# A one-layer streaming encoder with 32 experts: early expert chunks through GpSimd's queue, two engines in written order around the router, section sums beside the experts

## The chip, the cores and the metric

The kernel runs on one core of a Trainium2 chip. The metric is device time in microseconds of one execution, the median of three runs. All data are float32 in HBM at the start; the weights (some 500 MB) are read once, and one output of 256 x 2048 is written.

## The reference

One layer on 256 tokens of width 2048. A vector `c` gives six rows of 2048 (two shifts, two scales, two gates) through `silu(c) @ w_ada`. Then:

```
x <- x + g1 * ([mLSTM heads || RG-LRU blocks](rmsnorm(x)*(1+sc1) + sh1) @ w_out)
h  = rmsnorm(x)*(1+sc2) + sh2
x <- x + g2 * HierMoE(h)
y  = rmsnorm(x) * final_g
```

HierMoE picks for every token one of 4 groups by a softmax and 2 of its 8 experts by another; an expert is `(silu(h @ gate) * (h @ up)) @ down` with width 512 inside, 12 MB of weights. Only experts that got tokens are loaded: here 112 chunks of 1 MiB for each of the three matrices, 28 experts.

## The kernel before, in words

**Order.** TensorE and SyncE run in the order in which the code is written (`manual_schedule`). VectorE, ScalarE and GpSimd are ordered by a scheduler that estimates when inputs are there. Every engine works off its own list strictly in order: an instruction that waits holds all that stand behind it. SyncE issues nearly all weight loads, GpSimd only two loads of `x` and some clearing.

**Chunks.** Weights come in chunks of 1 MiB (128 partitions x 4 x 512) into seven `ring` buffers, later with three `more` and three `early` ones. `chunk` (line 154) takes the next buffer and puts the load on SyncE's queue, where it waits until the buffer's last reader is done. `weights` (line 168) makes the loads of one expert; its first three chunks go to the `early` buffers (lines 180 to 186): a pair that takes the place of `XG`, and one that takes the place of `va_aug`.

**Stages.** After the input projection (until about 435 us) comes the output projection `w_out`: 16 chunks, each split into two float32r halves by ScalarE and VectorE (lines 465, 466) and multiplied on TensorE (lines 495 to 497), four chunks for each quarter `n` of the 2048 columns. Beside it `ada_later` (line 303) works off w_ada for the later sections, chunk by chunk: most on VectorE (line 325, into `acc`), the last six on TensorE (line 315); `acc_sum` and `ada_sum` (lines 281 to 301) add up a section. `step` and `fill` hand out such side work. Just before the projection of `n` = 0 and 1 goes on with its second half, SyncE's list has the three `early` loads (line 832), and GpSimd loads `x` again into `X1` (line 829) for the residual.

**From the last residual to the first expert.** `residual` (776) adds to `X1` and sums squares; `router` (784) transposes the normed rows and multiplies with the router's weights; `fill` (853) does the last six w_ada chunks; `r2` is the norm (ScalarE's Sqrt, line 344); VectorE finds the group and both experts by maxima (lines 866 to 925, ends in `MS`); `choice_weights` (905) is two softmaxes with ScalarE's Exp; ScalarE writes the normed rows `XN` (933); TensorE counts (`pcnt`, `ppre`, lines 966 to 974), VectorE turns this into ranks (`key`, `cmp`, `hot`) and positions (`pre`, `pos0`, one-hot matrices `two`, lines 940 to 942). `gather` (945) multiplies `XN` with `two` and copies the result to `XE` in four pieces of four columns, VectorE and ScalarE in turn (lines 955, 958).

**Experts.** Ten rounds of two to four experts (`experts`, 1072). Round 0 has the two busiest experts and its tokens' positions are known before the full ranking is. In a round, `prod` (1089) does the gate and up products, chunk by chunk; each frees its buffer, and SyncE then loads the next chunk into it. `begin` (1229) is side work in round 0: the rest of the first gather, tables, `g2_rows`.

Of the kernel before, what the change touches and what calls it, by code (L numbers as in the profile page):

```python
# [14 lines left out]
OP = mybir.AluOpType  # L15
AX = mybir.AxisListType

D = 2048
# [21 lines left out]
NB = 1 + sum(n for _, n in OVER)  # L40
OVER_AFTER = 5

FILL = 5

EARLY = (2,)

# [63 lines left out]
def block_kernel(ctx, tc, x, c, w_ada, b_ada, w_in, b_gates, vec_a, vec_b, w_lru_a, w_lru_x, w_out,  # L110
# [57 lines left out]
    def weights(e, by_f, cond=None):  # L168
        cache = {}

        def f(part, kk):
            if (part, kk) not in cache:
                if part == 2 and by_f:
                    s = w_e_down[e].rearrange("a (f p) (j n) -> p (a f) j n", p=128, j=4)[:, kk]
                elif part == 2:
                    s = w_e_down[e].rearrange("a (f p) n -> p (a f) n", p=128)[:, :, kk * 512:kk * 512 + 512]
                else:
                    s = (w_e_gate, w_e_up)[part][e].rearrange("a (k p j) n -> p (a k) j n", p=128, j=4)[:, kk]
                count[0] += 1
                if count[0] == 1:  # L180
                    pair = st([128, 2, 4, 512], "early", "S1")
                    held.extend((pair[:, 0], pair[:, 1], st([128, 4, 512], "early3", "V8")))
                if count[0] <= 3:
                    cache[part, kk] = held[count[0] - 1]
                    SP.dma_start(cache[part, kk], s)
                    return cache[part, kk]
                if count[0] == 4:
                    more = st([128, 2, 4, 512], "more", "S4")
                    ring.extendleft(more[:, i] for i in range(2))
                    ring.extend(held)  # L190
                if count[0] == 6:
                    ring.appendleft(st([128, 4, 512], "more3", "ws", 3))
                cache[part, kk] = chunk(s, cond)
            return cache[part, kk]
        return f
# [644 lines left out]
    for n in (2, 3):  # L840
        ps = [pa() for _ in range(2)]
        for kk in (2, 3, 0):
            w_out_chunk(ps, n, kk)
        g1 = gate_row(n)
        w_out_chunk(ps, n, 1)
        if n == 3:
            drain()
        residual(ps, n, g1)
        if n == 2:
            side.append(router(n))  # L850


# [2 lines left out]
            step()  # L855
            next(later, None)

    for i, _ in enumerate(router(3)):
        if i == 1:
            fill()  # L860
    fill(FILL)
    ssum = st([128, 2], "ssum")
    V.tensor_reduce(ssum, ss2, axis=AX.X, op=OP.add)
    r2 = rstd_of(ssum, D, "r2")
    for h in range(2):
        V.scalar_tensor_tensor(lg[:, h], plg[:, h], r2[:, h:h + 1], shw, op0=OP.mult, op1=OP.add)

# [94 lines left out]

    for kk in range(4):
        normed(kk)
    pcnt = pb([128, 33], name="pcnt")
    for h in range(2):
        PE.matmul(pcnt[:, 0:32], ones, MS[:, h], start=h == 0, stop=h == 1)
    for h in range(2):
        PE.matmul(pcnt[:32, 32:33], MS[:, h], ones[:, 0:1], start=h == 0, stop=h == 1)
    ppre = pb([128, 2, 32])  # L970
    lt = cs[:, C_LT:C_LT + 128]
    PE.matmul(ppre[:, 0], lt, MS[:, 0], start=True, stop=True)
    PE.matmul(ppre[:, 1], lt, MS[:, 1], start=True, stop=False)
    PE.matmul(ppre[:, 1], ones, MS[:, 0], start=False, stop=True)
    cnt = small([33], "cnt")
    tcopy(cnt[:, 0:32], pcnt[:, 0:32])
    keyc = st([32, 1], "keyc")
# [3 lines left out]
    V.tensor_tensor(key, key, cs[:, C_KEY + 32:C_KEY + 64], op=OP.add)  # L981
    cmp = st([32, 32], "cmp")
    V.tensor_scalar(cmp, key[:32], keyc, None, op0=OP.is_lt)
    pre = small([2, 32], "pre")
    tcopy(pre, ppre)

    pre0, posx, pos0 = small([2, 2], "pre0"), small([2, 2, 2], "posx"), small([2, 2], "pos0")
    V.tensor_tensor(pre0, pre[:, :, 0:2], cs[:, None, C_B0:C_B0 + 2].to_broadcast([128, 2, 2]), op=OP.add)
    V.scalar_tensor_tensor(pre0, pre[:, :, 0:2], 64.0, pre0, op0=OP.is_lt, op1=OP.mult)
    for i in range(2):  # L990
        V.tensor_tensor(posx[:, i], Mf[:, i, :, 0:2], pre0, op=OP.mult)
    V.tensor_reduce(pos0, posx, axis=AX.X, op=OP.add)
    gather0 = gather(one_hot(lambda i, h: pos0[:, i, h:h + 1], 1))
    prk = pb([32, 32])
    PE.matmul(prk, ones[:32, :32], cmp, start=True, stop=True)
    hot = st([32, 32], "hot")
    V.tensor_scalar(hot, prk, cs[:32, C_P:C_P + 1], None, op0=OP.is_equal)
    XE = next(gather0)
    ptab = pb([128, 3, 32])
    for i in range(3):  # L1000
        PE.matmul(ptab[:, i], cs[:32, C_TAB + 128 * i:C_TAB + 128 * i + 128], hot, start=True, stop=True)
# [9 lines left out]
    for i in range(2):  # L1011
        V.tensor_tensor(pm2[:, i], Mf[:, i], posf, op=OP.mult)
    PW = small([2, 2, 2], "PW")
    V.tensor_reduce(PW[:, 0], pm2, axis=AX.X, op=OP.add)
    choice_weights()
    tcopy(PW[:, 1], wt)
    posr = small([4, NR], "posr")
    V.tensor_tensor(posr, PW[:, 0].rearrange("p i h -> p (i h)")[:, :, None].to_broadcast([128, 4, NR]),
                    cs[:, None, C_RB:C_RB + NR].to_broadcast([128, 4, NR]), op=OP.subtract)
    fill(16)  # L1020

    drain()
    g2 = st([128, D], "g2", "acc")

    def g2_rows(n):
        A.activation(g2[:, n * 512:n * 512 + 512], bcast(ada[:, 5, n * 4:n * 4 + 4]), AF.Copy)

    eidf = st([32, 2], "eidf")
    j32 = st([32, 32], "j32")
# [42 lines left out]
    def experts(members, XE, Cw, done=None, ahead=iter(()), before=iter(()), by_member=False):  # L1072
# [23 lines left out]
        def combine(n, pd):  # L1096
            ns = slice(n * 512, n * 512 + 512)
            C, sw = Cw
            y = w2([128, 512], "y")
            V.scalar_tensor_tensor(y, pd, sw, g2[:, ns], op0=OP.mult, op1=OP.mult)  # L1100
            ys = [w2([128, 512], f"ys{i}", F32R) for i in range(2)]
            A.activation(ys[0], y, AF.Copy)  # L1102
            V.tensor_tensor(ys[1], y, ys[0], op=OP.subtract)
# [98 lines left out]
            V.tensor_scalar(oslot, oslot, 128.0, None, op0=OP.add)  # L1202

    ss3 = st([128, 2, 4], "ss3")
    s3 = st([128, 2], "s3")
    fg = {}

    def final_row(n, t):
# [20 lines left out]
    def begin():  # L1229
# [4 lines left out]
        next(gather0)  # L1234
        yield
        tables()
        yield
        for n in range(4):
            g2_rows(n)
# [78 lines left out]
```

## Time and profile before

| what | value |
|---|---|
| median of 3 runs | 1372.88 us (1371.62, 1372.88, 5239.75) |
| profiled execution | 1371.18 us, span on the core 1369.4 us |
| busy share of the span | TensorE 85%, VectorE 40%, ScalarE 26%, GpSimd 0% |
| mean DMA rate | 369 GB/s over the span |
| DMA on the chain that ended last | 18% of the span, its largest part |

The span is from the first to the last instruction; the execution's own time has 1.8 us more around it. A share over the whole span hides that the stages have different limits: where TensorE is busy all the time the DMA queues pause, and the other way round, so the stages have to be read apart.

### The profile page before, as it was taken

What the parts mean: (1) busy time and instruction counts of PE and PEld (TensorE: products, weight loads), DVE (VectorE), ACT (ScalarE), POOL (GpSimd) and SP (SyncE); (2) the same over time, 40 slices, a digit from 0 to 9 for tenths busy, and PEclk for the clock granted to TensorE, in tenths of its full rate; (3) what the DMA queues carried; (4) which work ended last, traced back from release to release, by engine and by line L of the source; (5) the groups of instructions that cost most, each with busy time, mean ns of one, the idle gap of its engine ahead of it and who ended that gap; (6) DMA issues with size and microseconds to landing.
All of it is one profiled execution on the core that took longest, in us unless ns stands there. A gap on an engine that the chain in (4) does not pass through costs nothing. (4 is left out here: it accounts for less than half of the span.)

```text
span 1369.4 us, 20227 instructions
## 1 busy us (share of the span) xinstructions
PE 1170.4 (85%) x8186; PEld 682.6 (50%) x8186; DVE 545.6 (40%) x990; ACT 351.6 (26%) x562; POOL 4.0 (0%) x10
## 2 busy tenths in 40 slices
PE   4898999999999799699996878968885778887886
PEld 1666889988799678444431323313341133421432
DVE  1333666779769678422230131301331013130214
ACT  2233594545436344421010100101010010100103
POOL 0000000000000000000000000000000000000000
PEclk9999999999999899899999999999997899998998
DMA  9999869688968898879999999999997999999995
GB/s 337 367 356 364 269 225 346 243 319 316 400 250 330 343 376 324 338 286 389 423 422 423 424 423 423 423 424 422 423 423 320 423 423 424 422 423 424 423 414 218
DMA packets 116897, 504.84 MB, mean 369 GB/s; under 512 B 12424, under 2 KB 14760, under 8 KB 69184
## 3 DMA queue, kind: packets, MB, share of 16 engines
q1 hardware_dynamic: 115264, 500.11, 91.5%
q0 software_dynamic: 288, 2.10, 0.4%
q8 instruction: 66, 1.08, 0.3%
q10 hardware_dynamic: 1248, 1.29, 0.3%
q14 instruction: 31, 0.25, 0.0%
HBM read 526.54 MB, written 2.10 MB: 386 GB/s over the span
## 5 line engine op out<-in xcount | busy, mean ns | idle before, releaser
L1091 PE MATMUL pa<-ring,XE 128*32 128x512 f32 x1376 | 226.7, 630 | 56.8 <-DMA ring<-in_w_e_up_dram 28.5
L481 PE MATMUL pa<-HH,ws 128*128 128x256 f32 x640 | 189.6, 296 | 3.5 <-ACT ws L465 1.9
L483 PE MATMUL pa<-HH,ws 128*128 128x256 f32 x640 | 186.0, 291 | 5.2 <-DVE ws L466 5.2
L482 PE MATMUL pa<-HL,ws 128*128 128x256 f32 x640 | 185.8, 290 | 1.4 <-DVE HL L376 1.4
L466 DVE TENSOR_TENSOR ws<-ring,ws 128x1024 fp32r<-128x1024 f32 x128 | 154.6, 1220 | 70.1 <-ACT ws L465 65.4
L465 ACT ACTIVATE ws<-ring 128x1024 fp32r<-128x1024 f32 x128 | 134.1, 1058 | 171.9 <-PE pa L483 106.6
L1091 PE MATMUL pa<-early,XE 128*32 128x512 f32 x656 | 131.8, 622 | 25.9 <-DMA early<-in_w_e_up_dram 19.0
L1091 PEld LDWEIGHTS pa<-ring,XE 128*32 128x32 f32 x1376 | 60.3, 114 | 184.4 <-issue 99.0
L481 PEld LDWEIGHTS pa<-HH,ws 128*128 128x128 f32 x640 | 127.4, 199 | 19.6 <-issue 8.4
L483 PEld LDWEIGHTS pa<-HH,ws 128*128 128x128 f32 x640 | 127.3, 199 | 6.7 <-DVE ws L466 6.7
L482 PEld LDWEIGHTS pa<-HL,ws 128*128 128x128 f32 x640 | 127.4, 199 | 2.1 <-DVE HL L376 1.9
L955 ACT ACTIVATE XE<-pb,adx 128x128 f32<-128x128 f32 x80 | 36.6, 457 | 313.9 <-DVE XE L958 313.9
L1091 PE MATMUL pa<-more,XE 128*32 128x512 f32 x528 | 105.9, 609 | 12.8 <-DMA more<-in_w_e_up_dram 12.8
L1144 PE MATMUL pa<-ring,hT 128*32 128x512 f32 x616 | 102.1, 605 | 10.9 <-DMA ring<-in_w_e_down_dram 10.8
L1123 DVE TENSOR_TENSOR hs<-hs,pa 128x512 f32<-128x512 f32 x10 | 6.9, 688 | 260.9 <-PE pa L1091 260.9
L325 DVE SCALAR_TENSOR_TENSOR acc<-ring,cz,acc 128x1024 f32<-128x1024 f32 x80 | 100.3, 1277 | 0.8 <-DMA ring<-in_w_ada_dram 0.8
L1111 DVE TENSOR_TENSOR X<-X,pa 128x512 f32<-128x512 f32 x80 | 52.0, 683 | 93.9 <-PE pa L1109 93.9
L951 PE MATMUL pb<-two,XN 128*128 128x128 f32 x640 | 80.6, 286 | 8.0 <-ACT hT L1130 6.7
L951 PEld LDWEIGHTS pb<-two,XN 128*128 128x128 f32 x640 | 76.2, 198 | 19.4 <-issue 10.6
L1091 PEld LDWEIGHTS pa<-early,XE 128*32 128x32 f32 x656 | 32.0, 113 | 90.1 <-issue 41.8
L1102 ACT ACTIVATE ys<-y 128x512 fp32r<-128x512 f32 x40 | 25.2, 630 | 180.4 <-DVE y L1100 180.4
L1144 PE MATMUL pa<-more,hT 128*32 128x512 f32 x328 | 60.3, 594 | 5.4 <-DMA more<-in_w_e_down_dram 5.4
(369 smaller groups left out, 1267.5 us busy)
## 6 DMA issues: line engine op xcount, KB each, us to landing
ring<-in_w_ada_dram SPq DMA_DIRECT2D x96, 1024.0 KB
ring<-in_w_e_up_dram SPq DMA_DIRECT2D x61, 1024.0 KB
ring<-in_w_e_down_dram SPq DMA_DIRECT2D x60, 1024.0 KB
ring<-in_w_e_gate_dram SPq DMA_DIRECT2D x59, 1024.0 KB
ring<-in_w_in_dram SPq DMA_DIRECT2D x48, 1024.0 KB
early<-in_w_e_up_dram SPq DMA_DIRECT2D x30, 1024.0 KB
more<-in_w_e_down_dram SPq DMA_DIRECT2D x30, 1024.0 KB
more<-in_w_e_gate_dram SPq DMA_DIRECT2D x27, 1024.0 KB
```

What stands on the lines that cost most here:

```text
L325: V.scalar_tensor_tensor(o, w[:, h:h + 2], cz[:, k, 3:4], o, op0=OP.mult, op1=OP.add)
L465: A.activation(ws[:, 0], s, AF.Copy)
L466: V.tensor_tensor(ws[:, 1], s, ws[:, 0], op=OP.subtract)
L481: PE.matmul(o, wh[:, cc], HH[:, k], start=k == 0 and ch % 2 == 0, stop=False, skip_group_check=True)
L482: PE.matmul(o, wh[:, cc], HL[:, k], start=False, stop=False, skip_group_check=True)
L483: PE.matmul(o, wl[:, cc], HH[:, k], start=False, stop=k == 15, skip_group_check=True)
L951: PE.matmul(p[:, j], XN[:, h, kk, j], which[:, h], start=h == 0, stop=h == 1)
L955: A.activation(XE[:, k], p[:, j], AF.Identity, scale=adx[:, 1, k:k + 1], bias=adx[:, 0, k:k + 1])
L1091: PE.matmul(o[c0:c0 + width], lhs(kk, j)[:, c0:c0 + width], w[:, j], start=first and j == 0, stop=last and j == 3)
L1102: A.activation(ys[0], y, AF.Copy)
L1111: V.tensor_tensor(X1[:, h, ns], X1[:, h, ns], pc, op=OP.add)
L1144: PE.matmul(pds[n][c0:c0 + width], hT[:, f, c0:c0 + width], w[:, n], start=f == 0, stop=f == 3)
```

## The change

The first three expert chunks are issued by GpSimd in place of SyncE. The last `residual`, the last router quarter, the argmaxima, ranks, positions and choice weights are written out in a new order, and ScalarE and VectorE take that order as written (`in_order`); `choice_weights` moves behind the positions, `ppre` ahead of `pcnt`, the first one-hot ahead of the ranks. A Sqrt on a constant is written ahead of the last residual. Of the last six w_ada chunks four are worked off before the logits are scaled, two behind the counts (`FILL`). The sum of the last section (`acc_sum`, `ada_sum`) and the buffer `g2` move into `begin`, beside round 0.

```diff
--- before.py
+++ after.py
@@ -40,7 +40,7 @@
 NB = 1 + sum(n for _, n in OVER)
 OVER_AFTER = 5
 
-FILL = 5
+FILL = (4, 2)
 
 EARLY = (2,)
 
@@ -182,7 +182,7 @@
                     held.extend((pair[:, 0], pair[:, 1], st([128, 4, 512], "early3", "V8")))
                 if count[0] <= 3:
                     cache[part, kk] = held[count[0] - 1]
-                    SP.dma_start(cache[part, kk], s)
+                    G.dma_start(cache[part, kk], s)
                     return cache[part, kk]
                 if count[0] == 4:
                     more = st([128, 2, 4, 512], "more", "S4")
@@ -843,10 +843,8 @@
             w_out_chunk(ps, n, kk)
         g1 = gate_row(n)
         w_out_chunk(ps, n, 1)
-        if n == 3:
-            drain()
-        residual(ps, n, g1)
         if n == 2:
+            residual(ps, n, g1)
             side.append(router(n))
 
 
@@ -855,13 +853,32 @@
             step()
             next(later, None)
 
-    for i, _ in enumerate(router(3)):
-        if i == 1:
-            fill()
-    fill(FILL)
+    drain()
+    in_order = tc.manual_schedule(engines={mybir.EngineType.Activation, mybir.EngineType.DVE})
+    in_order.__enter__()
+
+    s3 = st([128, 2], "s3")
+    A.activation(s3, epsc, AF.Sqrt, scale=0.0, bias=eps)
+    residual(ps, 3, g1)
+    pxs = [pb([128, 2, S]) for _ in range(2)]
+    xts = [w2([128, 2, S], "xt") for _ in range(2)]
+    for i in range(2):
+        for j in range(2):
+            k = 12 + i * 2 + j
+            for h in range(2):
+                PE.transpose(pxs[i][:, j, h * 128:h * 128 + 128], X1[:, h, k * 128:k * 128 + 128], ident)
+    V.tensor_tensor(xts[0], pxs[0], ada[:, 4, 12:14, None].to_broadcast([128, 2, S]), op=OP.mult)
     ssum = st([128, 2], "ssum")
     V.tensor_reduce(ssum, ss2, axis=AX.X, op=OP.add)
     r2 = rstd_of(ssum, D, "r2")
+    for j in range(2):
+        A.activation(xts[1][:, j], pxs[1][:, j], AF.Copy, scale=ada[:, 4, 14 + j:15 + j])
+    for i in range(2):
+        for j in range(2):
+            for h in range(2):
+                PE.matmul(plg[:, h], xts[i][:, j, h * 128:h * 128 + 128], wr[:, 12 + i * 2 + j], start=False,
+                          stop=i == 1 and j == 1, skip_group_check=True)
+    fill(FILL[0])
     for h in range(2):
         V.scalar_tensor_tensor(lg[:, h], plg[:, h], r2[:, h:h + 1], shw, op0=OP.mult, op1=OP.add)
 
@@ -962,16 +979,27 @@
 
     for kk in range(4):
         normed(kk)
+    ppre = pb([128, 2, 32])
+    lt = cs[:, C_LT:C_LT + 128]
+    PE.matmul(ppre[:, 0], lt, MS[:, 0], start=True, stop=True)
+    PE.matmul(ppre[:, 1], lt, MS[:, 1], start=True, stop=False)
+    PE.matmul(ppre[:, 1], ones, MS[:, 0], start=False, stop=True)
     pcnt = pb([128, 33], name="pcnt")
     for h in range(2):
         PE.matmul(pcnt[:, 0:32], ones, MS[:, h], start=h == 0, stop=h == 1)
     for h in range(2):
         PE.matmul(pcnt[:32, 32:33], MS[:, h], ones[:, 0:1], start=h == 0, stop=h == 1)
-    ppre = pb([128, 2, 32])
-    lt = cs[:, C_LT:C_LT + 128]
-    PE.matmul(ppre[:, 0], lt, MS[:, 0], start=True, stop=True)
-    PE.matmul(ppre[:, 1], lt, MS[:, 1], start=True, stop=False)
-    PE.matmul(ppre[:, 1], ones, MS[:, 0], start=False, stop=True)
+    fill(FILL[1])
+    pre = small([2, 32], "pre")
+    tcopy(pre, ppre)
+
+    pre0, posx, pos0 = small([2, 2], "pre0"), small([2, 2, 2], "posx"), small([2, 2], "pos0")
+    V.tensor_tensor(pre0, pre[:, :, 0:2], cs[:, None, C_B0:C_B0 + 2].to_broadcast([128, 2, 2]), op=OP.add)
+    V.scalar_tensor_tensor(pre0, pre[:, :, 0:2], 64.0, pre0, op0=OP.is_lt, op1=OP.mult)
+    for i in range(2):
+        V.tensor_tensor(posx[:, i], Mf[:, i, :, 0:2], pre0, op=OP.mult)
+    V.tensor_reduce(pos0, posx, axis=AX.X, op=OP.add)
+    hot0 = one_hot(lambda i, h: pos0[:, i, h:h + 1], 1)
     cnt = small([33], "cnt")
     tcopy(cnt[:, 0:32], pcnt[:, 0:32])
     keyc = st([32, 1], "keyc")
@@ -981,21 +1009,12 @@
     V.tensor_tensor(key, key, cs[:, C_KEY + 32:C_KEY + 64], op=OP.add)
     cmp = st([32, 32], "cmp")
     V.tensor_scalar(cmp, key[:32], keyc, None, op0=OP.is_lt)
-    pre = small([2, 32], "pre")
-    tcopy(pre, ppre)
-
-    pre0, posx, pos0 = small([2, 2], "pre0"), small([2, 2, 2], "posx"), small([2, 2], "pos0")
-    V.tensor_tensor(pre0, pre[:, :, 0:2], cs[:, None, C_B0:C_B0 + 2].to_broadcast([128, 2, 2]), op=OP.add)
-    V.scalar_tensor_tensor(pre0, pre[:, :, 0:2], 64.0, pre0, op0=OP.is_lt, op1=OP.mult)
-    for i in range(2):
-        V.tensor_tensor(posx[:, i], Mf[:, i, :, 0:2], pre0, op=OP.mult)
-    V.tensor_reduce(pos0, posx, axis=AX.X, op=OP.add)
-    gather0 = gather(one_hot(lambda i, h: pos0[:, i, h:h + 1], 1))
+    gather0 = gather(hot0)
+    XE = next(gather0)
     prk = pb([32, 32])
     PE.matmul(prk, ones[:32, :32], cmp, start=True, stop=True)
     hot = st([32, 32], "hot")
     V.tensor_scalar(hot, prk, cs[:32, C_P:C_P + 1], None, op0=OP.is_equal)
-    XE = next(gather0)
     ptab = pb([128, 3, 32])
     for i in range(3):
         PE.matmul(ptab[:, i], cs[:32, C_TAB + 128 * i:C_TAB + 128 * i + 128], hot, start=True, stop=True)
@@ -1012,18 +1031,17 @@
         V.tensor_tensor(pm2[:, i], Mf[:, i], posf, op=OP.mult)
     PW = small([2, 2, 2], "PW")
     V.tensor_reduce(PW[:, 0], pm2, axis=AX.X, op=OP.add)
-    choice_weights()
-    tcopy(PW[:, 1], wt)
     posr = small([4, NR], "posr")
     V.tensor_tensor(posr, PW[:, 0].rearrange("p i h -> p (i h)")[:, :, None].to_broadcast([128, 4, NR]),
                     cs[:, None, C_RB:C_RB + NR].to_broadcast([128, 4, NR]), op=OP.subtract)
-    fill(16)
-
-    drain()
-    g2 = st([128, D], "g2", "acc")
+    choice_weights()
+    tcopy(PW[:, 1], wt)
+    in_order.__exit__(None, None, None)
+
+    g2 = []
 
     def g2_rows(n):
-        A.activation(g2[:, n * 512:n * 512 + 512], bcast(ada[:, 5, n * 4:n * 4 + 4]), AF.Copy)
+        A.activation(g2[0][:, n * 512:n * 512 + 512], bcast(ada[:, 5, n * 4:n * 4 + 4]), AF.Copy)
 
     eidf = st([32, 2], "eidf")
     j32 = st([32, 32], "j32")
@@ -1097,7 +1115,7 @@
             ns = slice(n * 512, n * 512 + 512)
             C, sw = Cw
             y = w2([128, 512], "y")
-            V.scalar_tensor_tensor(y, pd, sw, g2[:, ns], op0=OP.mult, op1=OP.mult)
+            V.scalar_tensor_tensor(y, pd, sw, g2[0][:, ns], op0=OP.mult, op1=OP.mult)
             ys = [w2([128, 512], f"ys{i}", F32R) for i in range(2)]
             A.activation(ys[0], y, AF.Copy)
             V.tensor_tensor(ys[1], y, ys[0], op=OP.subtract)
@@ -1202,7 +1220,6 @@
             V.tensor_scalar(oslot, oslot, 128.0, None, op0=OP.add)
 
     ss3 = st([128, 2, 4], "ss3")
-    s3 = st([128, 2], "s3")
     fg = {}
 
     def final_row(n, t):
@@ -1234,6 +1251,9 @@
         next(gather0)
         yield
         tables()
+        fill()
+        drain()
+        g2.append(st([128, D], "g2", "acc"))
         yield
         for n in range(4):
             g2_rows(n)
```

The order of instructions shows what becomes of it on three places. SyncE, where the output projection's second half begins (the difference; `ring` buffers are the chunks):

```order
 L158 DMA ring_65<-in_w_out_dram 128x4x512
 L158 DMA ring_66<-in_w_ada_dram 128x2048
-L185 DMA early<-in_w_e_gate_dram 128x2048 x2
-L185 DMA early_3863<-in_w_e_gate_dram 128x2048
 L158 DMA ring_67<-in_w_out_dram 128x4x512
 L158 DMA ring_68<-in_w_ada_dram 128x2048
```

The three `early` loads are gone from SyncE's list; the next `w_out` chunk follows at once. GpSimd after the change, from the clearing of `brow` to the branch after the rounds (`early_3863` is the buffer in `va_aug`'s place, `X_3859` is `X1`):

```order
L215 MEMSET brow 128x512 x4
L185 DMA early_3863<-in_w_e_gate_dram 128x2048
L185 DMA early<-in_w_e_gate_dram 128x2048
L829 DMA X_3859<-in_x_dram 128x2048 x2
L185 DMA early<-in_w_e_gate_dram 128x2048
L1208 TENSOR_LOAD on
```

Before, the two loads of `X1` stood alone there. Now two `early` loads stand ahead of them and one behind.

VectorE behind the choice of the experts, before (`MS` is the last of the choice, `gss` to `p` the choice weights):

```order
L925 TENSOR_TENSOR MS<-M 128x64
L886 TENSOR_REDUCE gss<-gp 128x2
L886 TENSOR_REDUCE ess<-ep 128x2
L887 RECIPROCAL gss<-gss 128x2
L887 RECIPROCAL ess<-ess 128x2
L888 TENSOR_TENSOR gp<-gp,gss 128x8
L888 TENSOR_TENSOR ep<-ep,ess 128x16
L910 TENSOR_REDUCE pg<-gp 128x2
L911 TENSOR_REDUCE p_4642<-ep 128x2
L912 TENSOR_TENSOR ept<-ep,h_4525 128x16
```

and after:

```order
L942 TENSOR_TENSOR MS<-M 128x64
L135 COPY pre<-pb 128x64
L997 TENSOR_TENSOR pre_4572<-pre,cs 128x4
L998 SCALAR_TENSOR_TENSOR pre_4572<-pre,pre_4572 128x4
L1000 TENSOR_TENSOR posx<-M,pre_4572 128x4 x2
L1001 TENSOR_REDUCE pos_4574<-posx 128x4
L958 TENSOR_SCALAR one<-cs,pos_4574 128x128
L959 SCALAR_TENSOR_TENSOR two<-cs,pos_4574,one 128x128
L958 TENSOR_SCALAR one<-cs,pos_4574 128x128
L959 SCALAR_TENSOR_TENSOR two<-cs,pos_4574,one 128x128
L135 COPY cnt<-pcnt 128x32
L1006 TENSOR_SCALAR keyc<-pcnt,cs 32x1
```

The softmax sums, which read ScalarE's Exp, stood right behind `MS`; now positions and one-hot matrices (`one`, `two`) stand there, and the ranks (`cnt`, `keyc`) behind them. The choice weights stand 36 rows behind `MS`, between copies of `XE`. The Sqrt on a constant (line 861) needs nothing that comes late, and stands on ScalarE right behind its first activation of the program, not at the last residual; the table load of line 344 is still there, now ahead of the second pair of `xt` copies, one of which pairs has moved to VectorE (line 870).

TensorE, from the ranks to the first expert, before (`acc` and `row` are the section's sum):

```order
L995 MATMUL pb<-cmp,cs 32x32
L951 MATMUL pb<-two,XN 128x128 x8
L1001 MATMUL pb<-hot,cs 128x32 x3
L285 MATMUL pa<-acc,cs 32x512 x4
L298 MATMUL pb<-cs,row 128x4 x4
L951 MATMUL pb<-two,XN 128x128 x8
L1091 MATMUL pa<-early,XE 32x512 x16
```

and after:

```order
L968 MATMUL pb<-two,XN 128x128 x8
L1015 MATMUL pb<-cmp,cs 32x32
L1020 MATMUL pb<-hot,cs 128x32 x3
L968 MATMUL pb<-two,XN 128x128 x8
L1109 MATMUL pa<-early,XE 32x512 x16
L968 MATMUL pb<-two,XN 128x128 x8
```

The section's sum is gone from here (it now stands in round 0 behind the third pair of gate chunks and the tables), and the first gather stands ahead of the rank's product.

## Rows read from the trace of the kernel before

**Rows 1.** the page, a group: busy us, mean ns; idle before, releaser.

```profile
L955 ACT ACTIVATE XE<-pb,adx 128x128 f32<-128x128 f32 x80 | 36.6, 457 | 313.9 <-DVE XE L958 313.9
```

**Rows 2.** busy time by stretch (us): engines (xcount), then PEclk, DMA share, GB/s.

```profile
442.50:445.00 2.50, 2.50 (x14) 2.08 (x13) 2.32 (x5) 1.86 (x3) 0.00 (x0) 1.00 0.01 3
460.00:468.00 8.00, 0.65 (x4) 0.20 (x2) 0.03 (x1) 1.12 (x2) 0.00 (x0) 0.69 1.03 424
553.00:586.00 33.00, 22.39 (x144) 15.27 (x144) 15.67 (x88) 16.11 (x23) 0.00 (x0) 0.74 0.71 290
575.00:590.00 15.00, 14.12 (x90) 10.09 (x91) 5.35 (x25) 1.83 (x4) 0.00 (x0) 0.75 0.12 51
710.00:1040.00 330.00, 258.50 (x1816) 99.34 (x1812) 70.01 (x146) 29.04 (x56) 0.00 (x0) 0.95 1.01 421
```

**Rows 3.** SyncE's queue in order of time: start us, us, what.

```profile
449.30 1.28 SPq L185 DMA_DIRECT2D early<-in_w_e_gate_dram  x3
450.63 0.64 SPq L158 DMA_DIRECT2D ring<-in_w_out_dram  x1
...
589.66 5.88 SPq L158 DMA_DIRECT2D early<-in_w_e_up_dram  x3
```

**Rows 4.** what SyncE's queue waited for: us in total, times, longest us.

```profile
SPq L185 <- PE pb L656: 10.6, 1, 10.6
```

**Rows 5.** TensorE in order of time, output projection; in brackets idle before, releaser.

```profile
467.99 0.79 PE L495 MATMUL pa<-ws,YM 128*128 128x512 f32 x1 [7.35 <-ACT ws L465]
...
473.52 0.39 PE L495 MATMUL pa<-ws,YM 128*128 128x512 f32 x1
...
476.29 0.60 PE L338 MATMUL pb<-cs,ada 128*128 128x128 f32 x4
...
483.66 0.50 PE L497 MATMUL pa<-ws,YM 128*128 128x512 f32 x1 [0.85 <-DVE ws L466]
```

**Rows 6.** DMA issues: count, KB each, median us from issue to landing.

```profile
X<-in_x_dram POOLq DMA_DIRECT2D x2, 1024.0 KB, 10.6
```

**Rows 7.** TensorE in order of time, from the router to the first experts.

```profile
574.78 3.75 PE L951 MATMUL pb<-two,XN 128*128 128x128 f32 x16 [1.30 <-DVE two L942]
578.46 1.16 PE L1001 MATMUL pb<-hot,cs 32*128 32x32 f32 x6
579.55 1.07 PE L285 MATMUL pa<-acc,cs 128*32 128x512 f32 x8
581.50 1.06 PE L298 MATMUL pb<-cs,row 128*128 128x4 f32 x8 [0.88 <-DVE row L292]
582.42 3.64 PE L951 MATMUL pb<-two,XN 128*128 128x128 f32 x16
585.99 3.64 PE L1091 MATMUL pa<-early,XE 128*32 128x512 f32 x32
589.56 2.05 PE L951 MATMUL pb<-two,XN 128*128 128x128 f32 x16
```

**Rows 8.** ScalarE in order of time, same stretch.

```profile
555.71 0.84 ACT L795 ACTIVATE xt<-pb,ada 128x256 f32<-128x256 f32 x2
556.57 1.28 ACT L344 ACT_TABLE_LOAD   x1
...
568.48 1.28 ACT L884 ACT_TABLE_LOAD   x1
```

**Rows 9.** VectorE in order of time, same stretch.

```profile
560.43 0.42 DVE L866 SCALAR_TENSOR_TENSOR lg<-pa,r,shw 128x36 f32<-128x36 f32 x2 [2.08 <-PE pa L802]
...
565.00 0.23 DVE L925 TENSOR_TENSOR MS<-M 128x64 f32<-128x64 f32 x1
570.02 0.16 DVE L886 TENSOR_REDUCE gss<-gp 128x2 f32<-128x8 f32 x1 [4.79 <-ACT gp L884]
...
572.16 0.18 DVE L135 COPY cnt<-pcnt 128x32 f32<-128x32 f32 x1
...
574.30 0.60 DVE L942 SCALAR_TENSOR_TENSOR two<-cs,pos,one 128x128 f32<-128x128 f32 x2
```


## The prediction, made before the changed kernel ran

> **What bounds the kernel now.** I read the page, then the busy time by stretch, then the three engines and SyncE's queue in order of time where a stretch showed idle DMA. All is one profiled execution, 1371.2 us, of which 1369.4 are the span; the median of the three runs, 1372.9, is 1.7 above it. The sum is made against 1371.2.
>
> Most of the second half is the experts' weights. From 710 to 1040 us the DMA queues are full all the time, 421 GB/s, and TensorE is busy for 258.5 of 330 us [rows 2]. There nothing that an engine does counts; the end is the time at which this stream begins, plus its bytes. What counts is therefore when the buffers begin to come free for it, and where DMA stood still before. It does so twice.
>
> The first place is in the output projection: from 442.5 to 445 us the queues move 3 GB/s, while TensorE has no idle time [rows 2]. SyncE waits there 10.6 us for one thing, the buffer pair of the first expert chunks, which TensorE's line 656 still reads [rows 4]. Not until 449.30 does it issue these loads and, right behind them, the next chunk of w_out [rows 3]. The price comes 15 us later: TensorE sits 7.35 us until 467.99 because that chunk is late [rows 5], and DMA runs at full rate meanwhile [rows 2].
>
> The second place is the router. From 575 to 590 us the queues move 51 GB/s [rows 2], which against 421 is 13.2 us of standstill: all buffers hold chunks of round 0, and the next load waits until the first pair of them is used, at 589.66 [rows 3, 7]. In the 33 us from 553 to 586 TensorE is busy for 22.4 and its mean granted clock is 0.74 [rows 2]. The chain goes logits (560.43), choice (to 565.23), then VectorE waits 4.79 us for an Exp of the choice weights [rows 9], because ScalarE writes eight normed pieces first and then loads a table, at 568.48 [rows 8]; then the choice weights, ranks and positions follow, and the first gather starts at 574.78 [rows 7].
>
> **Term 1: early chunks through GpSimd.** SyncE's list loses three loads and their wait. When it comes free in the trace it issues the next w_out chunk only 0.05 us after the early ones [rows 3], so a buffer was free for it; in the change it goes out when SyncE reaches it, some 10 us earlier, into queues that stand still. It was 7.4 us late; so it is there in time. What TensorE gets back: the 7.35 us; the half clock behind that wait (the first 12 matmuls take 467.99 to 473.52, 5.53 us, the second 12 take 2.77 [rows 5], so 2.8 us); and the 0.85 us at 483.66, where a split stood behind the residual on VectorE and now stands ahead of it [rows 5]. Together 11.0 us. GpSimd's queue pays: `X1` is loaded behind one early chunk. The nearest row is `X1` itself, two loads that landed after 10.6 us beside a full SyncE queue [rows 6]; a third at the same pace, 15.9 us from 449.3, ends at 465, and the residual that needs `X1` begins some 11 us earlier than in the trace, after 472. So this stays hidden, with about 7 us to spare. Lower end of the term: only the issue time of 1.28 us [rows 3]; upper end 11.0, since nothing else of TensorE's is idle there. I take 11.0, since the idle queues and the wait are both in the rows.
>
> For this I weighed a rule. The Trainium skill ("DMA: Bandwidth & Descriptors", section "Issuing engines are not separate DMA queues") says that loads issued from several engines run on the same 16 DMA engines, and that starting them elsewhere saves only the time of issue, usually small. Here the rows disagree as to what is saved: the issue is small, but the wait ahead of it held a whole list.
>
> **Term 2: from the last residual to the first expert.** Four steps.
> (a) Logits. The table load of the norm ran at 556.57, behind two copies of router columns, 0.84 us [rows 8]. In the new order it stands right behind the squares, and one pair of copies is VectorE's. The second pair, and with it the last router product, is earlier by about that, and 0.2 more since nothing stands between: the logits come at 559.4 in place of 560.43, 1.0. That the Sqrt on a constant ends up at the start of the program costs and brings nothing here, as the load no longer stands behind anything; I set it to 0.
> (b) Choice to one-hot. Before, 9.7 us lie between the end of `MS` (565.23) and the end of the one-hot (574.90) [rows 9]: 4.79 waiting, 2.1 of choice weights, 2.7 from the first copy of the counts at 572.16 on [rows 9]. Now the wait and the choice weights are behind. What is left: the `ppre` product, which now comes first on TensorE, 1.0, and of the 2.7 about 2.5, as the rank's steps no longer lie between. 3.5 in place of 9.7: 6.2.
> (c) Clock. Both gathers before the first expert took 3.75 and 3.64 us; the third one, of the same size, took 2.05 [rows 7], because TensorE had sat idle before the rank product and the granted clock was low (0.75 from 575 to 590 [rows 2]). Without the long wait TensorE has w_ada products and counts to fill the time, and I take 2.05 for both: 1.7 and 1.6.
> (d) The section's sum (1.07, a wait of 0.88, 1.06 [rows 7]) no longer stands there: 3.0. Against it: the table product (1.16 [rows 7]) now waits for `hot`, which VectorE makes behind two copies of `XE`, and for the first gather's buffer, free after four copies; these go in turn at 0.46 [rows 1], 1.9 in all, with only the short rank product beside them: costs 1.7.
> Sum 1.0 + 6.2 + 3.3 + 1.3 = 11.8: the first expert matmul comes 21.2 in place of 33.0 us after the last w_out one. Bounds: without the clock 8.5. Upwards DMA ends it: its standstill of 13.2 us [rows 2] is all that can be won.
>
> **Term 3: the section's sum beside round 0.** It stands behind the third pair of gate chunks, so TensorE frees the later buffers 2.1 us later, plus a wait for the row, 0.9 as before: 3.0 [rows 7]. The queues are nearly, but not always, busy there, so it can be hidden in part; 0 to 4, I take 2.9. The choice weights' place in VectorE's list, between copies of `XE`, I set to 0: a piece of `XE` is wanted one pair of products (3.64) and one gather (2.05) [rows 7] after its own gather, and its copies (1.9), one-hot steps (1.1) and a table load of 1.28 [rows 8] fit into that.
>
> **Sum.** 1371.2 - 11.0 - 11.8 + 2.9 = 1351.3; a median lies a little above a profile here, so I say 1352. From the ends: 11.0 + 13.2 - 0 gives 1347.0; 1.3 + 8.5 - 4 gives 1365.4. Two per cent, about what one takes as a clear difference here, is 27.5 us.
>
> **Rivals.**
> *The rule holds* (only issue time saved; the bytes are the limit). The early chunks and `X1`, 5 MB, then still stand ahead of w_out's chunks. Then 1371.2 - 1.3 - 8.9 = 1361. For it: behind 450 us DMA is full for long. Against: 3 GB/s before [rows 2]. 0.15. This is what the rule of the Trainium skill ("DMA: Bandwidth & Descriptors") in term 1 comes to.
> *The choice weights come back on the path.* VectorE and ScalarE are bound to the written order; softmax, Exp and copies of `XE` wait for each other, and TensorE waits in round 0 for `XE`. Price: up to the 6.9 us of before (4.79 and 2.1 [rows 9]), less the spare time of 1.4: 5.5. 1357. For it: two engines, one list each, a table load between two copies. 0.12.
> *Slower.* `X1` starves. Its loads stand on GpSimd's queue behind an early chunk and beside SyncE's full queue; if they land late, VectorE stops at the residual's addition (line 781), and behind it stand the splits for which TensorE waits. Every us after 472 is lost, and from 20 us on, a landing after 492, the kernel is slower than before; 25 us late gives 1376, and slower by 2% needs 47. A landing at 492 means 14 us a load, where two took 10.6 [rows 6]. The Trainium skill ("DMA: Bandwidth & Descriptors", section "SWDGE vs HWDGE vs iDMA") says that GpSimd writes its descriptors into SBUF, out of which VectorE's two-port mode locks it; no row shows that it held the two loads of before. 0.04, and 0.02 of it beyond 2%.
> *It does not do what it says:* the chain is limited elsewhere, for instance a clock that stays low, and DMA finds its standstill again; 1364 to 1372. 0.04.
> *More than I see:* the section's sum is hidden, and round 0 runs without DMA pauses; below 1345.4, over 2% faster. 0.05.
> The forecast, 1347 to 1357, has 0.60.
>
> So the range is 1346 to 1361.5: it leaves out the slow cases, the largest gain and half of the first rival. Faster by over 2%: 0.05, rounded up to 0.06 for what I may have mis-sized; slower by over 2%: 0.02; within: 0.92.
>
> **What would show it.** Term 1: no DMA standstill at 442.5 to 445 of the length of before, no TensorE wait of 7 us for a w_out chunk, the last w_out matmul at about 542 in place of 553. Term 2: the first expert matmul about 21 us behind it, the choice weights' sums behind the one-hot, both gathers at about 2 us. Term 3: lines 285 and 298 in round 0 with a short wait between. Wrong would be: VectorE stopping at line 781 until `X1` lands; TensorE waiting for `XE` in round 0; or DMA idle as long as before ahead of the first freed buffer.

## The result, and the profile after

The changed kernel takes 1352.51 us (median of four runs, 1352.37 to 1355.04), the kernel before 1371.62 beside it (median of three runs, 1371.36 to 1372.88; a fourth, of 5239.75 us, is left out here, but was counted in the median of 1372.88 us at the start). The ratio of the times is 0.9863, with a 95% interval from 0.9843 to 0.9882. It is 19.1 us or 1.4% faster: measurable, and under the 2% of a clear difference. The profiled execution has a span of 1350.3 us, 19.1 less than before. I forecast 1352.

The total alone says little on why. I cut the span at three events that stand in every trace: SyncE issues the first w_out load, the last w_out matmul starts (line 497), and SyncE issues the first load into a freed `early` buffer (the last row of [rows 3]). SyncE's queue of the changed kernel in order of time (start us, us, what):

```profile
414.10 0.38 SPq L158 DMA_DIRECT2D ring<-in_w_out_dram  x1
...
432.40 0.43 SPq L158 DMA_DIRECT2D ring<-in_w_out_dram  x1
...
566.56 5.88 SPq L158 DMA_DIRECT2D early<-in_w_e_up_dram  x3
```

The load at 432.40 is the w_out chunk that stood behind the three early loads, at 450.63 in [rows 3]: counted from the first w_out load it goes out 14.9 us sooner. The same queue before, and TensorE's last w_out row before:

```profile
417.40 0.38 SPq L158 DMA_DIRECT2D ring<-in_w_out_dram  x1
```

```profile
552.61 0.39 PE L497 MATMUL pa<-ws,YM 128*128 128x512 f32 x1
```

| stretch | before | after | difference | forecast |
|---|---|---|---|---|
| A: start to the first w_out load | 417.4 | 414.1 | -3.3 | 0 |
| B: to the last w_out matmul | 135.2 | 125.2 | -10.0 | -11.0 (term 1) |
| C: to the first freed buffer | 37.05 | 27.2 | -9.8 | -11.8 (term 2) |
| D: to the end of the span | 779.7 | 783.7 | +4.0 | +2.9 (term 3) |

**B.** TensorE has no wait of 7 us any more; before, that was the first row of [rows 5]. GpSimd's queue (start us, us, what; in brackets idle before, releaser):

```profile
409.11 0.66 POOL L185 DMA_DIRECT2D early<-in_w_e_gate_dram  x1 [34.72 <-ACT ws L465]
446.26 0.53 POOL L185 DMA_DIRECT2D early<-in_w_e_gate_dram  x1 [36.49 <-DVE TO L657]
448.74 1.05 POOL L829 DMA_DIRECT2D X<-in_x_dram  x2 [1.95 <-DVE YM L659]
```

GpSimd stands 36.5 us for the buffer pair, and nobody waits for GpSimd. SyncE issues w_out chunks meanwhile, and the standstill of [rows 2] (3 GB/s) is gone, as the busy time by stretch shows (length, engines with xcount, then PEclk, DMA share, GB/s):

```profile
440.00:445.00 5.00, 5.00 (x25) 4.08 (x25) 5.00 (x9) 3.01 (x6) 0.00 (x0) 1.00 0.82 283
445.00:450.00 5.00, 5.00 (x26) 4.12 (x25) 5.00 (x10) 2.92 (x4) 1.79 (x4) 1.00 1.03 393
...
540.00:545.00 5.00, 3.35 (x15) 2.86 (x16) 2.78 (x6) 3.77 (x9) 0.00 (x0) 0.71 1.00 423
545.00:550.00 5.00, 5.00 (x27) 2.79 (x30) 2.42 (x13) 5.00 (x5) 0.00 (x0) 0.50 0.49 208
```

Before, the standstill filled a whole stretch of this length:

```profile
445.00:450.00 5.00, 5.00 (x27) 4.15 (x26) 5.00 (x10) 3.05 (x5) 0.00 (x0) 1.00 0.01 3
```

w_out chunks are still late at ScalarE, which splits them, three times and 9.0 us in all, but TensorE has earlier chunks to multiply. The longest of the three:

```profile
465.46 1.06 ACT L465 ACTIVATE ws<-ring 128x1024 fp32r<-128x1024 f32 x1 [4.33 <-DMA ring<-in_w_out_dram]
```

**C and D.** TensorE from the end of w_out on, the answer to [rows 7]:

```profile
539.33 0.39 PE L497 MATMUL pa<-ws,YM 128*128 128x512 f32 x1
540.71 0.30 PE L869 MATMUL pb<-cs,X 128*128 128x128 f32 x1 [0.99 <-DVE X L781]
541.95 1.63 PE L869 MATMUL pb<-cs,X 128*128 128x128 f32 x7 [0.94 <-DVE X L781]
543.50 3.63 PE L879 MATMUL pa<-wr,xt 128*128 128x36 f32 x16
547.07 6.25 PE L315 MATMUL pa<-ring,cz 128*32 128x512 f32 x32
553.24 0.41 PE L984 MATMUL pb<-MS,cs 128*128 128x32 f32 x2
...
556.43 2.05 PE L968 MATMUL pb<-two,XN 128*128 128x128 f32 x16
...
560.13 0.85 PE L1020 MATMUL pb<-hot,cs 32*128 32x32 f32 x6 [1.48 <-DVE hot L1017]
560.91 2.05 PE L968 MATMUL pb<-two,XN 128*128 128x128 f32 x16
562.90 3.64 PE L1109 MATMUL pa<-early,XE 128*32 128x512 f32 x32
...
578.74 1.06 PE L285 MATMUL pa<-acc,cs 128*32 128x512 f32 x8
580.78 1.03 PE L298 MATMUL pb<-cs,row 128*128 128x4 f32 x8 [0.97 <-DVE row L292]
```

And VectorE there, the answer to [rows 9]:

```profile
547.17 0.42 DVE L883 SCALAR_TENSOR_TENSOR lg<-pa,r,shw 128x36 f32<-128x36 f32 x2 [2.72 <-PE pa L879]
...
551.74 0.22 DVE L942 TENSOR_TENSOR MS<-M 128x64 f32<-128x64 f32 x1
554.13 0.22 DVE L135 COPY pre<-pb 128x64 f32<-128x64 f32 x1 [2.18 <-PE pb L986]
...
565.47 0.16 DVE L903 TENSOR_REDUCE gss<-gp 128x2 f32<-128x8 f32 x1 [0.56 <-ACT gp L901]
```

The choice weights are behind the one-hot now (565.47), both gathers take 2.05 us in place of 3.75 and 3.64, and lines 285 and 298 stand in round 0. But there is something new: from 545 to 550 us TensorE's clock is at the lower of its two levels (0.50), and the four w_ada chunks of line 315 take 6.25 us for 32 matmuls, whereas 16 of them cost 1.9 at the full clock. They last until 553.2. `MS` is ready at 551.96, and the prefix product (line 984), for which VectorE waits 2.18 us, stands behind them.

DMA's standstill ahead of the first freed buffer is nearly gone: in the 15 us up to it the queues moved 60 GB/s before and 393 now. A shorter one is new: from 547.5 to 550 us they move nothing, since SyncE waits up to 11.1 us for `ring` buffers that line 315 reads at the low clock.

### The profile page after: what moved, and what is told of

It reads as the page before. It is cut to its first block, busy times and chain, and to the rows that moved or that the text cites. A ratio compares the mean times of both kernels' runs of the same rounds, so it can differ in the third digit from the quotient of the medians.

```text
span 1350.3 us, 20232 instructions
## 1 busy us (share of the span) xinstructions
PE 1166.2 (86%) x8186; PEld 678.3 (50%) x8186; DVE 547.7 (41%) x991; ACT 351.4 (26%) x561; POOL 5.6 (0%) x13
## 5 line engine op out<-in xcount | busy, mean ns | idle before, releaser
L968 PE MATMUL pb<-two,XN 128*128 128x128 f32 x640 | 77.3, 279 | 6.7 <-ACT hT L1148 6.7
L968 PEld LDWEIGHTS pb<-two,XN 128*128 128x128 f32 x640 | 73.1, 192 | 18.9 <-issue 9.2
```

Of the source, the lines that this page charges most:

```text
L968: PE.matmul(p[:, j], XN[:, h, kk, j], which[:, h], start=h == 0, stop=h == 1)
```

## The experiments

All twelve in the four stretches, from one profile each (us), with the ratio to the kernel before from the timed runs:

| kernel | A | B | C | D | ratio, 95% interval |
|---|---|---|---|---|---|
| before | 417.4 | 135.2 | 37.05 | 779.7 | |
| before, second profile | 417.0 | 135.2 | 37.0 | 780.3 | 1.0000 (0.9988 to 1.0012) |
| changed | 414.1 | 125.2 | 27.2 | 783.7 | 0.9863 (0.9843 to 0.9882) |
| changed, second profile | 414.5 | 125.2 | 27.2 | 783.5 | 0.9870 (0.9855 to 0.9886) |
| 1 GpSimd alone | 416.05 | 125.2 | 35.7 | 781.0 | 0.9894 (0.9878 to 0.9910) |
| 2 SyncE again | 416.1 | 135.3 | 27.2 | 783.3 | 0.9946 (0.9932 to 0.9959) |
| 3 no early Sqrt | 415.1 | 125.3 | 27.2 | 784.7 | 0.9878 (0.9863 to 0.9893) |
| 4 early Sqrt alone | 417.2 | 135.2 | 37.0 | 780.1 | 1.0005 (0.9996 to 1.0013) |
| 5 sum ahead | 416.7 | 125.2 | 32.5 | 781.0 | 0.9888 (0.9873 to 0.9903) |
| 6 choice first | 414.3 | 125.25 | 36.1 | 783.15 | 0.9930 (0.9917 to 0.9944) |
| 7 fill ahead | 417.6 | 125.25 | 26.7 | 784.8 | 0.9863 (0.9848 to 0.9878) |
| 8 sum in the gap | 417.6 | 125.2 | 27.1 | 781.75 | 0.9856 (0.9841 to 0.9871) |
| 9 fill before the choice | 414.0 | 125.5 | 29.0 | 784.0 | 0.9870 (0.9855 to 0.9885) |
| 10 fill and sum | 415.1 | 125.3 | 24.85 | 782.1 | 0.9844 (0.9826 to 0.9862) |

Where the program of a whole stretch is the same, B and C repeat within 0.4 us and D within 1.6. So B and C tell single microseconds apart, which D and the medians do not.

**1. GpSimd alone**, on the kernel before:

```diff
-                    SP.dma_start(cache[part, kk], s)
+                    G.dma_start(cache[part, kk], s)
```

> The kernel before with one edit: GpSimd issues the three early expert chunks. Theory (the wait ahead of the chunks held SyncE's whole list): TensorE's wait of 7.35 us for a w_out chunk is gone, the last w_out matmul ends some 10 us earlier, the first expert matmul still comes 33 us after it, and the kernel is 10 us faster, ratio 0.993. Rival (only the time of issue is saved, the bytes still stand ahead of w_out's chunks): 1.3 us, ratio 0.999. Rival (the gain is given back in the standstill of DMA from 575 to 590 us): TensorE's wait goes, the time stays, ratio 1.000.

1357.47 us against 1371.49. B is 10.0 shorter, as in the changed kernel, and C stays near that of before (1.4 shorter; the wait for the Exp is 2.79 us in place of the 4.79 of [rows 9], because the scheduler now puts VectorE's copies of the counts ahead of the choice weights, which the one line changed as well). The theory holds: the spans differ by 11.5 us, -10.0 in B, -1.4 each in A and C, +1.3 in D. (The medians differ by 14.0; the profiled run is the slowest of its five.) DMA's standstill of [rows 2] doesn't take the gain back.

**2. SyncE again**, on the changed kernel: the same line, the other way.

> The changed kernel with one edit undone: SyncE issues the three early chunks again. Theory (the parts add up): TensorE waits again some 7 us for a w_out chunk, w_out ends some 10 us later, the first expert matmul still comes 23.5 us behind it, and the kernel is 10 us slower than the changed one, 0.993 of the kernel before. Rival (the early chunks decide only the issue time): 1 us slower than the changed one, 0.987.

1363.76 us. B is back at 135.3, C and D are those of the changed kernel. TensorE's two waits of [rows 5] are back:

```profile
466.53 0.79 PE L495 MATMUL pa<-ws,YM 128*128 128x512 f32 x1 [7.25 <-ACT ws L465]
482.38 0.50 PE L497 MATMUL pa<-ws,YM 128*128 128x512 f32 x1 [0.85 <-DVE ws L466]
```

So the parts add up, and the first is worth 10.0 by both runs. The Trainium skill's rule ("DMA: Bandwidth & Descriptors", section "Issuing engines are not separate DMA queues"), that another issuing engine saves the issue time alone, would have given 1.3; these traces differ from it by what stood behind the wait.

**3 and 4. Without the early Sqrt, and that alone.** Stretch A came out 3.3 us shorter, though nothing of the change was meant for it; the one instruction that moved there is the Sqrt on a constant.

```diff
-    A.activation(s3, epsc, AF.Sqrt, scale=0.0, bias=eps)
```

> The changed kernel without the Sqrt on a constant, which runs at the program's start. In the changed kernel's trace all work up to the first w_out load is already 3.3 us earlier than before. Theory A (this Sqrt does it: its table is loaded while ScalarE idles, and the norm of the input comes 1.3 us less late): w_out's first load is issued at 417.4 us in place of 414.1, and the kernel is 3 us slower than the changed one, 0.989 of the kernel before. Theory B (the stretches of half clock in the input projection fall as they fall): 414.1 or anything between, unrelated to this edit.

> The kernel before with one edit: the Sqrt on a constant at the program's start. Theory A (this Sqrt brings the 3.3 us): w_out's first load is issued at 414.1 us in place of 417.4, and the kernel is 3 us faster, ratio 0.998. Theory B (chance of the clock): no difference from before, ratio 1.000, or one that does not match the edit.

Without it A is 415.1, not 417.4; alone it gives 417.2 and 1371.84 us, the time of before. The Sqrt is not the cause.

**The two kernels again**, unaltered.

> The changed kernel itself, unaltered, profiled and timed a second time beside the next two. Eight kernels whose input projection is the same, or differs by one early Sqrt, issued the first w_out load anywhere from 414.1 to 417.6 us. Theory (half-clock stretches fall differently from execution to execution): this profile lies elsewhere than 414.1 in that range, by up to 3.5 us, while the time from that load to the end stays at 936 within 1 us. Rival (the place belongs to the program): 414.1 again.

> The kernel before, unaltered, profiled a second time. The changed kernel's two profiles issued the first w_out load at 414.1 and 414.5 us, the kernel before at 417.4, its copy with an early Sqrt at 417.2. Theory (the place belongs to the program): 417.4 again, within 0.5. Rival (chance of the execution): anywhere from 414 to 417.6. By both, from that load on to the end 952 us, within 1 us.

Both repeat their A within 0.5 us (414.5 and 417.0), and the rest within 0.6. That speaks for A as a property of the program, but two profiles each do not show it, as timed runs of one kernel spread wider (before from 1367.99 to 1374.36 us). Against it, the changed kernel and runs 2 and 5 to 10 have the same instructions in the same order on every engine up to there, and lie between 414.0 and 417.6. All but about 1 us of the difference arises in the first 130 us. In the four programs with the latest A (before, and runs 4, 7 and 8) TensorE's clock from 66 to 74 us is 0.79 on the mean; it is 1.00 in the others, except for run 6. What decides it stays open.

**5. Sum ahead**: the last section's sum and `g2` back ahead of the experts.

```diff
+    fill()
+    drain()
+    g2 = [st([128, D], "g2", "acc")]
     choice_weights()
...
-        fill()
-        drain()
-        g2.append(st([128, D], "g2", "acc"))
```

> The changed kernel with the last section's sum (and the buffer g2) back ahead of the experts, behind the positions. Theory (the sum in round 0 holds up buffers by its 3.06 us and they are lost at the end): the first expert matmul comes 4.2 us later, round 0 runs 3.06 us shorter, and the kernel is 1.2 us slower than the changed one. Rival (beside round 0 the sum was hidden by DMA): the whole 4.2 us are lost.

D is 2.7 us shorter, C 5.3 longer; 1356.5 us. The theory holds in kind: what the sum takes in round 0 is paid for at the end. Its price ahead of the experts was higher than its own 3 us: the clock is low from the sum on (0.50 from 561.43 to 566 us), and TensorE then waits for the row:

```profile
548.73 4.82 PE L315 MATMUL pa<-ring,cz 128*32 128x512 f32 x32
...
556.95 2.05 PE L968 MATMUL pb<-two,XN 128*128 128x128 f32 x16
...
561.43 1.93 PE L285 MATMUL pa<-acc,cs 128*32 128x512 f32 x8
564.53 1.84 PE L298 MATMUL pb<-cs,row 128*128 128x4 f32 x8 [1.17 <-DVE row L292]
566.23 3.76 PE L968 MATMUL pb<-two,XN 128*128 128x128 f32 x16
```

Up to the sum this run has the lists of the changed kernel on every engine, and yet the first gather starts 15.02 us after the last w_out matmul (541.93), not 17.10. The clock in between is 0.89 on the mean, in the changed kernel 0.70, and the four w_ada chunks take 4.82 us in place of 6.25. VectorE's logits and `MS` of this run:

```profile
548.84 0.42 DVE L883 SCALAR_TENSOR_TENSOR lg<-pa,r,shw 128x36 f32<-128x36 f32 x2 [1.78 <-PE pa L879]
...
553.41 0.23 DVE L942 TENSOR_TENSOR MS<-M 128x64 f32<-128x64 f32 x1
```

**6. Choice first**: the choice weights ahead of the first one-hot.

```diff
     fill(FILL[1])
+    choice_weights()
...
-    choice_weights()
```

> The changed kernel with the choice weights back ahead of the first one-hot (behind the counts, in the written order). Theory: VectorE waits for the Exp, which stands behind the eight normed pieces on ScalarE until 553.9 and a table load of 1.28 us; with 2.1 us of its own the copy of the prefix counts comes at 557.6 in place of 554.1, so the first expert matmul is 3.5 us later and the kernel 3.5 us slower than the changed one. Rival (the longer idle time of TensorE brings the half clock back to both gathers, 1.6 us each): 6.7 us slower. Rival (hidden, the queues are full anyway): no difference.

1361.49 us, C 8.9 longer: more than either. Both happen. The copy of the prefix counts comes 4.0 us later behind `MS`, and then TensorE, which waited 3.59 us, does the gathers and the first experts at the low clock (1.9, 1.7 and 1.0 us more than in the changed kernel):

```profile
560.30 3.91 PE L968 MATMUL pb<-two,XN 128*128 128x128 f32 x16 [3.59 <-DVE two L959]
...
567.27 3.78 PE L968 MATMUL pb<-two,XN 128*128 128x128 f32 x16
570.99 4.63 PE L1109 MATMUL pa<-early,XE 128*32 128x512 f32 x32
```

**7. Fill ahead**: two of the four w_ada chunks go where TensorE waits for the residual.

```diff
-FILL = (4, 2)
+FILL = (2, 2, 2)
...
     residual(ps, 3, g1)
+    fill(FILL[2])
```

> The changed kernel with two of the four w_ada chunks moved from behind the router's products to ahead of its last transposes, where TensorE waits for the residual from 539.7 to 541.9 us. Theory (those chunks hold up the prefix counts): the prefix product starts as soon as MS is there, 1.3 us earlier, the kernel is 1.3 us faster than the changed one; up to 2 us more if TensorE's clock stays up from 540 to 553. Rival (DMA, not this chain, sets the end): no difference.

1353.7 us, no difference. The prefix counts are copied 1.24 us after `MS` in place of 2.39, as expected, and the logits come 0.95 earlier; but C is only 0.5 shorter. TensorE now waits 1.93 us for `MS`, its clock falls behind that, and the last two chunks hold up the gather until 559.49, some 1.5 us behind the end of the one-hot. B, C and D together are 936.8 us, in the changed kernel 936.2:

```profile
554.70 0.38 PE L985 MATMUL pb<-MS,cs 128*128 128x32 f32 x2 [1.93 <-DVE MS L943]
...
556.44 3.11 PE L315 MATMUL pa<-ring,cz 128*32 128x512 f32 x13
559.49 2.05 PE L969 MATMUL pb<-two,XN 128*128 128x128 f32 x16
```

**8. Sum in the gap**: line 285 into TensorE's wait for `hot`, and the row ahead of the choice weights.

```diff
     PE.matmul(prk, ones[:32, :32], cmp, start=True, stop=True)
+    acc_sum()
...
+    step()
+    step()
     choice_weights()
```

> The changed kernel with the last section's sum on TensorE (line 285) in the wait of 1.48 us for the rank's one-hot, and its row and transposition ready before round 0 needs them. Theory (round 0's sum is paid for at the end): 1.06 us of products and 0.97 us of wait leave round 0, the kernel is 2.0 us faster than the changed one. Rival (hidden beside DMA): no difference.

D is 2.0 us shorter, the theory's number and somewhat more than D's scatter. The median, 1352.34 us, doesn't show it: A of this program is 3.5 later.

**9. Fill before the choice**: as 7, with `FILL = (4, 0, 2)`, so that no chunk stands behind the counts.

> As the run with two w_ada chunks ahead of the last transposes, but the last two, which stood behind the counts, now stand with the other two behind the router's products. Theory (those two held up the first gather there: 3.11 us at a low clock, until 559.5, when the one-hot was done at 557.4): the gather starts at the end of the one-hot, the first expert matmul comes 146.2 us after the first w_out load in place of 148.8, and the kernel is 2.5 us faster than the changed one. Rival (TensorE's idle time only moves, and with it the half clock onto the gathers, 1.6 us each): no gain, or up to 1 us slower. Rival (four chunks at half clock last 6.2 us and hold up the prefix product as before): no difference.

1354.72 us, C 1.8 longer than in the changed kernel: the first rival. The gather begins at 554.15, within 0.5 us of the end of the one-hot, and could not have begun sooner: it waits for the last normed piece, `XN`, which ScalarE ends at 554.10. TensorE has two idle waits here. The clock falls ahead of the second, within the first gather (0.75 on the mean from 554.15 to 557.20 us), and everything up to the first experts is slow:

```profile
554.15 3.06 PE L969 MATMUL pb<-two,XN 128*128 128x128 f32 x16 [1.31 <-ACT XN L951]
...
558.86 1.49 PE L1021 MATMUL pb<-hot,cs 32*128 32x32 f32 x6 [1.41 <-DVE hot L1018]
560.28 3.78 PE L969 MATMUL pb<-two,XN 128*128 128x128 f32 x16
```

**10. Fill and sum**: 9 and 8 together.

> The run before this one together with the section's sum in the wait for the rank's one-hot. Theory (both gains add): 2.5 and 2.0, together 4.5 us faster than the changed kernel, ratio to the kernel before 0.983. Rival (only the sum's 2.0 hold, since w_ada chunks merely move the low clock): 2.0, ratio 0.985. Rival (the first freed buffer no longer sets the end): no difference from the changed kernel, 0.986.

1349.52 us, the fastest: 4.3 below the changed kernel beside it. The two intervals overlap, but C and D point the same way: 2.4 and 1.4 us less, the latter within D's scatter. The sum in the gap leaves round 0, it shortens the second wait, and the clock stays up:

```profile
554.80 2.38 PE L969 MATMUL pb<-two,XN 128*128 128x128 f32 x16 [1.32 <-DVE two L960]
...
557.29 1.07 PE L285 MATMUL pa<-acc,cs 128*32 128x512 f32 x8
558.83 0.85 PE L1022 MATMUL pb<-hot,cs 32*128 32x32 f32 x6 [0.48 <-DVE hot L1019]
559.61 2.05 PE L969 MATMUL pb<-two,XN 128*128 128x128 f32 x16
```

The same five microseconds, in run 9 and then in run 10:

```profile
555.00:560.00 5.00, 3.59 (x22) 3.23 (x20) 1.76 (x9) 0.92 (x2) 0.00 (x0) 0.57 1.00 421
```

```profile
555.00:560.00 5.00, 4.40 (x35) 3.12 (x35) 2.64 (x14) 0.92 (x2) 0.00 (x0) 1.00 1.02 428
```

That the sum keeps the clock up is not shown by this. Up to the sum both runs have the same lists on every engine and first waits of 1.31 and 1.32 us, and the gather behind that wait, ahead of the sum, took 3.06 us at the falling clock in run 9 and 2.38 at 1.00 here. So the clock differed before the programs did, and run 10's gain in C is at least in part its clock.

## Why the prediction was right, and where it was not

The time was right to within a microsecond, the terms less so: 19.9 us were forecast from terms 1 to 3, and 15.8 are there in B to D. The rest came from A, of which I had forecast nothing: 3.3 us that made the total right by luck.

**Term 1** was right: the wait, not the issue, was the price, and w_out's chunks go out while the queues are free. I said 11.0; it is 10.0. At 470 us all of it was there: matmul by matmul, counted from the first w_out load, TensorE was 11.5 us ahead of the kernel before. Then 1.5 us were lost, because the clock falls once more (0.75 on the mean from 485 to 490 us), with no wait of TensorE ahead of it. The w_out matmuls there start 0.42 us apart, the same ones before 0.23; first the changed kernel, then before:

```profile
488.22 0.63 PE L497 MATMUL pa<-ws,YR 128*128 128x512 f32 x1
488.64 0.63 PE L495 MATMUL pa<-ws,YR 128*128 128x512 f32 x1
```

```profile
502.75 0.40 PE L497 MATMUL pa<-ws,YR 128*128 128x512 f32 x1
502.98 0.40 PE L495 MATMUL pa<-ws,YR 128*128 128x512 f32 x1
```

All ten profiles with GpSimd's early loads have this fall, the four with SyncE's do not; why stays open. The rival of the rule is refuted by runs 1 and 2. `X1` didn't starve: it was issued at 448.74, such a load took 10.5 us, and VectorE's addition at 470.32 had no wait before it.

**Term 2** went as described, 2.0 us short, and what is short is the clock. (a) The logits were to come 1.0 earlier; they come 7.84 us behind the last w_out row, before 7.82. The table load does follow the squares at once, at 542.67, but TensorE was at the low clock, and the 16 router products took 3.63 us.

(b) From `MS` to the first gather I forecast 6.2 less, and it is 5.1 (4.69 in place of 9.78): the step that failed is that `ppre` would cost 1.0 since it "comes first on TensorE". First of its kind, yes, but four w_ada chunks at half clock were ahead of it. I counted them in (c) as what keeps the clock up, and did not ask how long they last if it is down.

Run 5, whose clock held better over the same lists, has both steps as I forecast them: logits 6.91 us behind the last w_out row, 0.9 earlier than before, and 3.54 us from `MS` to the first gather, 6.2 less. The other five profiles with these lists have 7.8 to 8.0 and 4.5 to 4.8, so run 5 is the exception, and what decides between the two is not shown.

(c, d) From the first gather to the first expert 4.7 us were won where I said 4.6: both gathers ran at 2.05. Run 10 has C at 24.85, 12.2 less than before, so the 11.8 were there to be had, with another distribution of the same chunks, the sum in the gap, and a clock that held; run 9, with the same order up to that sum, has 29.0. Runs 5 and 6 price two parts of the order, low clock included: the sum ahead of the experts costs 5.3 us in C, the choice weights 8.9.

**Term 3** was 2.9; the seven profiles with the whole sum in round 0 have D from 783.15 to 784.8, mean 783.9, the five without it 779.7 to 781.0, mean 780.4: 3.5, within the 0 to 4 given. Runs 5 and 8, which take the sum out of round 0, have D shorter by 2.7 and 2.0, where its products and its wait take 3.1: DMA hides little of it. The choice weights cost nothing in their new place, as I said: TensorE doesn't wait for `XE` in round 0, and that rival is refuted.

**The Sqrt** I set at 0, and run 4 shows 0.

## What to carry to other kernels

A wait at the head of a list costs what stands behind it; if another engine's list is idle, a load that must wait belongs there. Filling work for idle TensorE time is sized at the low clock: four chunks took 6.25 us here where a better clock gave 4.82, and the product that ends the chain stood behind them. Moving that work was no gain by itself (C 0.5 us shorter in run 7, 1.8 longer in run 9). When a change moves several things, cut the trace at events that all versions have: the totals here mixed 15.8 us of effect with 3.3 that the change didn't explain.

## What the runs showed of the hardware

A short wait of TensorE did not decide by itself what its clock did next. Behind a wait of 1.31 us the granted clock fell in run 9 (0.75 from 554.15 to 557.20 us), behind one of 1.32 us with the same lists it stayed at 1.00 in run 10. Behind a wait of 1.47 us it fell in run 5 (0.50 from 561.43 to 566 us), behind one of 1.48 us with the same lists it stayed at 1.00 in the changed kernel. Gathers at the fallen clock of run 9 took 1.0 and 1.7 us longer.

Programs with the same lists on all engines differed by up to 3.6 us in the first 414 us, while two profiles of one program agreed within 0.5. Nothing in these runs says what decides it.
